# Six more weight units get their low parts by an accumulating DMA, and the causal weights are loaded later

## The chip, the cores and the metric

The kernel runs on one core of one Trainium2 chip. The metric is the device time of one execution in microseconds (us). Engines are called by these names: PE or TensorE (matmul), DVE or VectorE, ACT or ScalarE, POOL or GpSimd, SP or SyncE (here only a queue that issues DMAs).

## What is computed

Two layers of an autoregressive decoder trunk, for 512 prompt positions and 8 single-step samples side by side (T = 520 columns), 1024 channels. Layer 0 is a conv module, layer 1 a chunked gating module; after each comes `x <- LayerNorm(alpha * x + sublayer(x))`. What matters here is the end of layer 0 and the start of layer 1:

```python
# end of layer 0
y = concat([a, bo]) * silu(g)
out = einsum('bld,de->ble', y, w_out_ab)          # second half of it: z_p
x = layer_norm(alpha * x + out, ln_g[0], ln_b[0])
# layer 1
z = einsum('bld,de->ble', x, w_in_c)
u, v, g = split(z)
u = gelu(u); v = layer_norm(gelu(v))
w_causal = w_s * tril(ones((128, 128)))           # the causal weights, 8 heads
mix = einsum('hts,bnshd->bnthd', w_causal, v_in_chunks) + b_s
y = u * mix * silu(g)
out = einsum('bld,de->ble', y, w_out_c)
x = layer_norm(alpha * x + out, ln_g[1], ln_b[1])
```

## The kernel before

Activations lie with channels on the 128 partitions: eight tiles of 128 x 520 for 1024 channels. All matmul operands are split in two float32r parts, a high one (rounded) and a low one (what the rounding left), and each product is three matmuls: hi x hi, lo x hi, hi x lo. So 8 channel tiles (k) by 3 make the 24 matmuls of one output tile of 128 x 260.

The weights come as "units" of 1024 x 128, 512 KB each, in the order of use, through `unit(n)`, which loads ahead up to five units (`LEAD`). `load_unit` (lines 116 to 129) does for each: SP issues the load of `raw` (three buffers), ScalarE makes the high part `whi` (L121), and the low part `wlo` is made in one of two ways. Either VectorE subtracts `raw - whi` (L128), or, for units in the set `BY_DMA` (10 to 49 before), ScalarE writes `-raw`, rounded, into `wlo` (L125) and GpSimd issues a DMA that reads the unit from memory a second time and adds it to `wlo` on the way (L126). `whi` and `wlo` lie in 12 buffers, six units; units 70 and 71 lie in the buffers of tag `M` instead.

The place of this change:

- Units 64 to 71 are the last part of layer 0's output projection (`z_p`). `out_part` (line 478) runs over them twice, first for columns 0 to 259, then for columns 260 to 519, called at lines 587 and 588. In it, for each of eight output tiles, VectorE adds the sums to the residue `r` (L492) and with that frees the PSUM bank. After the fourth, a matmul with ones (`shift`, L502) gives a first mean, which VectorE subtracts from all eight `r` (L504); squares (ScalarE L507) and sums follow, and `norm()` closes it: means by matmul (L384, L385, `mean` and `sqs`), L536 to L538 for the reciprocal deviation, L544, L566, ScalarE's L567. `split_x1` (line 577) makes the parts `x1h` (ScalarE L582) and `x1l` (VectorE L583) for layer 1. The first columns' norm lies beside the second columns' matmuls.
- Units 72 to 77 are the first six v units of layer 1 (`NVF` = 6). They are also done twice: `z_v{i}_0` for the first columns (line 627), which lies beside the second columns' norm, then `z_v{i}_1` (line 633). Both take PSUM banks in turn with `z_p`, by `one()`. Units 78 to 87 are the other v units, over all columns at once.
- Between the two stands the code for the causal weights: loads of `wt` and `bs` by GpSimd's queue, the causal mask (`affine_select`), and the split into `wth` and `wtl` on GpSimd. `wth` and `wtl` are first read by the matmuls `rows` (L674), `wt` by `mix` (L718), `bs` by VectorE's L713; all come after the v units.

The order of the instructions on each engine is set by a scheduler from the program's order, its own model of durations, and the priorities in the code (`soon()`, `background()`); each engine then runs its list in order. GpSimd's list holds its DMA issues too.

Of the kernel before, what the change touches and what calls it, by code (L numbers as in the profile page):

```python
# [9 lines left out]
F32 = mybir.dt.float32  # L10
F32R = mybir.dt.float32r
BF16 = mybir.dt.bfloat16
AF = mybir.ActivationFunctionType
ALU = mybir.AluOpType
AX = mybir.AxisListType

P = 128
D = 1024
E2 = 2048
SEQ = 512  # L20
# [8 lines left out]
NH = 8  # L29
# [21 lines left out]
def decoder_kernel(  # L51
# [19 lines left out]
    nc = tc.nc  # L71
# [3 lines left out]
    wpool = ctx.enter_context(tc.tile_pool(name="wpool", bufs=1))  # L75
# [9 lines left out]
    def y_slot(dt, name, n=T):  # L85
        return slots.tile([P, n], dt, tag="Y", name=name, bufs=17)

    def ab_slot(name):
        return slots.tile([P, T], F32, tag="AB", name=name, bufs=8)
# [7 lines left out]
    def zt(name):  # L97
        return zps.tile([P, 2, 512], F32, tag="z", name=name)

    def mt(name):  # L100
        return mps.tile([P, 512], F32, tag="m", name=name)

    def zh(z):
        return z[:, :, :TH]

    def two(t):
        return t.rearrange("p (a b) -> p a b", a=2)

    def hs(h):
        return slice(h * TH, (h + 1) * TH)  # L110
# [5 lines left out]
    def load_unit(wtag=("W", 12)):  # L116
# [5 lines left out]
        lo = wpool.tile([P, KT, P], F32R, tag=wtag[0], name=f"wlo_{n}", bufs=wtag[1])  # L122
        if n in BY_DMA:

# [4 lines left out]
        units.append((hi, lo))  # L129


    BY_DMA = set(range(10, 50))
    EXTRA = set()
    for base in (64, 128):
        EXTRA.update((base + 6, base + 7))
# [1 line left out]
    def unit(n):  # L137
        while len(units) < min(n + 1 + LEAD, n_units):
            load_unit(("M", 4) if len(units) in EXTRA else ("W", 12))
        return units[n]  # L140

    def mm(ps, w, ah, al, c):
        hi, lo = w
        for k in range(KT):
            for j, (a, b) in enumerate(((hi, ah), (lo, ah), (hi, al))):
                nc.tensor.matmul(  # L146
                    ps,
                    a[:, k, :],
                    b[k][:, c],
                    start=(k == 0 and j == 0),  # L150
                    stop=(k == KT - 1 and j == 2),
                )

    def halves(z):
        return [z[:, h, :] for h in range(2)]

    def mm2(z, w, ah, al):
        hi, lo = w
        for k in range(KT):
            for h in range(2):  # L160
                for j, (a, b) in enumerate(((hi, ah), (lo, ah), (hi, al))):
                    nc.tensor.matmul(  # L162
                        z[h][:, :TH],
                        a[:, k, :],
                        b[k][:, hs(h)],
                        start=(k == 0 and j == 0),
                        stop=(k == KT - 1 and j == 2),
                    )
# [15 lines left out]
    for k in range(KT):  # L184
# [5 lines left out]
        q, j = k // 4, k % 4  # L190
# [64 lines left out]
    def one(j, name):  # L255
        if j % 2:
            return zt(name)[:, 0, :]
        return cps.tile([P, SEQ], F32, tag="cv", name=name)
# [29 lines left out]
    for i in range(KT):  # L288
# [64 lines left out]
        op=ALU.mult,  # L353
# [5 lines left out]
    with background():  # L359
        for j in range(2):  # L360
# [6 lines left out]
                op=ALU.mult,  # L367
# [209 lines left out]
    def split_x1(d, c0, c1):  # L577
# [11 lines left out]
    n += KT  # L589


    wt = wpool.tile([P, NH, P], F32, tag="M", name="wt", bufs=4)
    nc.gpsimd.dma_start(wt, wsT_in)
    bs = wpool.tile([P, NH, P], F32, tag="M", name="bs", bufs=4)
    nc.gpsimd.dma_start(bs, bs_in)

    nc.gpsimd.affine_select(
        wt, wt, pattern=[[0, NH], [1, P]], compare_op=ALU.is_ge, fill=0.0, base=0, channel_multiplier=-1
    )

    wth, wtl = [], []
    for j in range(2):
        w = wt[:, 4 * j : 4 * j + 4, :].rearrange("p a b -> p (a b)")
        wth.append(y_slot(F32R, f"wth_{j}", SEQ))
        wtl.append(y_slot(F32R, f"wtl_{j}", SEQ))
        nc.gpsimd.tensor_copy(wth[j], w)
        nc.gpsimd.tensor_tensor(wtl[j], w, wth[j].bitcast(F32), op=ALU.subtract)

    NV = 2 * KT
    NVF = 6  # L610
    vt = [None] * NV
# [4 lines left out]
    def v_tok(i):  # L616
        nc.gpsimd.tensor_copy(vs[:, i, :], vt[i][:, SEQ:])
        m = mt(f"vt_{i}")
        for c in range(NC):
            nc.tensor.transpose(m[:, c * P : (c + 1) * P], vt[i][:, c * P : (c + 1) * P], ident)  # L620
        t = ab_slot(f"vtok_{i}") if i < 8 else slots.tile([P, T], F32, tag="SB", name=f"vtok_{i}", bufs=8)
        nc.scalar.copy(t[:, :SEQ], m)
        for c in range(NC):
            nc.vector.bn_stats(stats[:, c, i, :], t[:, c * P : (c + 1) * P])
        vtok[i] = t
# [7 lines left out]
    for i in range(NVF):  # L633
        z = one(i, f"z_v{i}_1")[:, :TH]
        mm(z, unit(n + i), x1h, x1l, hs(1))
        t = vt[i]
        with tc.issue_after(last_act[0]):
            nc.scalar.activation(t[:, hs(0)], t[:, hs(0)], AF.Gelu_apprx_tanh)
        nc.scalar.activation(t[:, hs(1)], z, AF.Gelu_apprx_tanh)
        if i > 0:  # L640
            v_tok(i - 1)
    for i in range(NVF, NV):
        z = zt(f"z_v{i}")
        mm2(halves(z), unit(n + i), x1h, x1l)
        vt[i] = y_slot(F32, f"v_{i}")
        nc.scalar.activation(two(vt[i]), zh(z), AF.Gelu_apprx_tanh)
        v_tok(i - 1)
# [244 lines left out]
```

## Time and profile before

| what | us |
|---|---|
| median of 3 runs | 834.26 (833.76 to 834.76) |
| the profiled execution | 834.73 |
| its span, first to last instruction | 833.0 |
| TensorE busy | 814.2 (98%) |
| VectorE busy | 536.6 (64%) |
| ScalarE busy | 347.2 (42%) |
| GpSimd busy | 88.0 (11%) |

Rows of the profile read: place in the span or source line, engine, operation, what is written from what, shapes, count, then busy us and mean ns. In the list of waits: who waited, for whom, total us, times, longest. In a timeline: start, length, and in brackets the idle time ahead of it and what ended it. TensorE overlaps its matmuls, so the time per matmul is read from one start to the next, not from the length of one.

### The profile page before, as it was taken

Reading aid. Unit: us, or ns where it says so; the run is one execution under the profiler, and the core shown is the slowest. Engines: PE = TensorE matmul, PEld = TensorE weight load, DVE = VectorE, ACT = ScalarE, POOL = GpSimd, SP = SyncE. Lnnn points to the kernel's source line nnn. Section 1 sums busy time; section 2 is a strip of 40 time slices with the busy share of each in tenths; the row PEclk is TensorE's granted clock in tenths of the full one; section 3 lists DMA queues with packets and bytes.
Section 4 is the critical chain, followed back from the end, with each engine's and each line's share of the span. In section 5 each row is a group of like instructions: output and inputs, shape, how many; then the busy total and the mean of one; then the engine's idle time right before and its main releaser. Section 6 shows DMA issues by size and latency. Waiting matters only on the chain.

```text
span 833.0 us, 16028 instructions
## 1 busy us (share of the span) xinstructions
PE 814.2 (98%) x6792; PEld 812.2 (98%) x6792; DVE 536.6 (64%) x914; ACT 347.2 (42%) x510; POOL 88.0 (11%) x158
## 2 busy tenths in 40 slices
PE   8999999999999999999989999999999999999994
PEld 8999999999999999999979999999999999999993
DVE  5899998999962576446885432596355433526566
ACT  5545454455354444442647423323432133334243
POOL 0121221221110000000021111100000000000032
PEclk9999999999999999999989999999999999999997
DMA  8798988889888543231331432214233223222011
GB/s 290 208 206 191 209 185 185 184 191 216 182 173 189 167 115 102 79 124 52 84 119 51 128 85 93 77 56 126 78 87 92 84 94 102 77 87 92 1 53 52
DMA packets 32873, 103.37 MB, mean 124 GB/s; under 512 B 4209, under 2 KB 7937, under 8 KB 32801
## 3 DMA queue, kind: packets, MB, share of 16 engines
q1 hardware_dynamic: 26000, 79.01, 32.2%
q0 software_dynamic: 6800, 23.33, 15.0%
q8 instruction: 53, 0.87, 0.4%
q14 instruction: 20, 0.16, 0.1%
HBM read 98.89 MB, written 3.44 MB: 123 GB/s over the span
## 4 chain that ended last, share of the span: by engine, by line
PE 96%; DMA 1%; DVE 1%; ACT 0%; SPq 0%; issue 0%; ACTq 0%; DVEq 0%
PE z_p L146 11%; PE z_gc L162 11%; PE z_u L162 11%; PE z_v L162 7%; PE z_q L162 6%; PE z_o L162 6%; PE z_c L162 5%; PE z_ga L162 5%; PE z_post L162 5%; PE z_h L162 5%; PE z_gb L162 5%; PE z_val L162 5%; PE z_gate L162 5%; PE z_v L146 5%; PE mix L718 2%; PE vt L620 1%
## 5 line engine op out<-in xcount | busy, mean ns | idle before, releaser
L121 ACT CAST whi<-raw 128x1024 fp32r<-128x1024 f32 x134 | 139.9, 1048 | 324.9 <-PE z_u L162 44.9
L128 DVE TENSOR_TENSOR wlo<-raw,whi 128x1024 fp32r<-128x1024 f32 x94 | 114.4, 1224 | 142.5 <-ACT whi L121 141.9
L274 DVE SCALAR_TENSOR_TENSOR acc<-apad,pa,acc 128x512 f32<-128x512 f32 x240 | 165.7, 751 | 3.6 <-ACT acc L271 2.7
L162 PE MATMUL z_gc<-x1h,whi 128*128 128x260 f32 x256 | 72.9, 285 | 0.0
L162 PE MATMUL z_u<-x1h,whi 128*128 128x260 f32 x256 | 72.4, 283 | 0.0
L162 PE MATMUL z_gc<-x1h,wlo 128*128 128x260 f32 x256 | 72.0, 281 | 0.0
L162 PE MATMUL z_u<-x1l,whi 128*128 128x260 f32 x256 | 72.0, 281 | 0.0
L162 PE MATMUL z_gc<-x1l,whi 128*128 128x260 f32 x256 | 72.0, 281 | 0.0
L162 PE MATMUL z_u<-x1h,wlo 128*128 128x260 f32 x256 | 72.0, 281 | 0.0
L126 POOL DMA_DIRECT2D wlo<-in_wu x40 | 34.7, 869 | 139.2 <-ACT wlo L125 132.2
L162 PEld LDWEIGHTS z_u<-x1h,wlo 128*128 128x128 f32 x256 | 48.1, 188 | 0.1
L162 PEld LDWEIGHTS z_gc<-x1h,wlo 128*128 128x128 f32 x256 | 48.2, 188 | 0.0
L162 PEld LDWEIGHTS z_gc<-x1l,whi 128*128 128x128 f32 x256 | 48.1, 188 | 0.0
L162 PEld LDWEIGHTS z_u<-x1h,whi 128*128 128x128 f32 x256 | 48.0, 188 | 0.1
L162 PEld LDWEIGHTS z_u<-x1l,whi 128*128 128x128 f32 x256 | 48.1, 188 | 0.0
L162 PEld LDWEIGHTS z_gc<-x1h,whi 128*128 128x128 f32 x256 | 48.1, 188 | 0.0
L162 PE MATMUL z_v<-x1h,whi 128*128 128x260 f32 x160 | 46.0, 287 | 0.0
L162 PE MATMUL z_v<-x1h,wlo 128*128 128x260 f32 x160 | 45.0, 281 | 0.0
L162 PE MATMUL z_v<-x1l,whi 128*128 128x260 f32 x160 | 45.0, 281 | 0.0
L125 ACT ACTIVATE wlo<-raw 128x1024 fp32r<-128x1024 f32 x40 | 42.2, 1055 | 0.0
L162 PE MATMUL z_c<-xh,wlo 128*128 128x260 f32 x128 | 36.1, 282 | 0.3 <-DVE wlo L128 0.3
L146 PE MATMUL z_p<-yh_c,whi 128*128 128x260 f32 x128 | 36.3, 284 | 0.0
(260 smaller groups left out, 2723.4 us busy)
## 6 DMA issues: line engine op xcount, KB each, us to landing
raw<-in_wu SPq DMA_DIRECT2D x134, 512.0 KB, 3.9
wlo<-in_wu POOLq DMA_DIRECT2D x40, 512.0 KB, 7.7
xr<-in_xT SPq DMA_DIRECT2D x8, 260.0 KB, 4.2
x<-in_xT SPq DMA_DIRECT2D x7, 260.0 KB, 5.1
out_y<-r SPq DMA_DIRECT2D x8, 130.0 KB, 1.7
out_y<-out SPq DMA_DIRECT2D x4, 260.0 KB, 2.2
raw_s<-in_w SPq DMA_DIRECT2D x8, 128.0 KB, 4.5
xs<-in_cache_a SPq DMA_DIRECT2D x2, 496.0 KB, 8.2
```

What stands on the lines that cost most here:

```text
L121: nc.scalar.copy(hi, raw)
L125: nc.scalar.mul(lo, raw, -1.0)
L126: nc.gpsimd.dma_start(lo, wu[n - 2], accum_op=ALU.add)
L128: nc.vector.tensor_tensor(lo, raw, hi.bitcast(F32), op=ALU.subtract)
L146: nc.tensor.matmul(ps, a[:, k, :], b[k][:, c], start=(k == 0 and j == 0), stop=(k == KT - 1 and j == 2),)
L162: nc.tensor.matmul(z[h][:, :TH], a[:, k, :], b[k][:, hs(h)], start=(k == 0 and j == 0), stop=(k == KT - 1 and j == 2),)
L274: nc.vector.scalar_tensor_tensor(acc[i], apads[i][:, j : j + SEQ], pa[:, i, PA_W + j : PA_W + j + 1], acc[i], op0=ALU.mult, op1=ALU.add,)
L620: nc.tensor.transpose(m[:, c * P : (c + 1) * P], vt[i][:, c * P : (c + 1) * P], ident)
L718: nc.tensor.matmul(m[:, c * P : (c + 1) * P], vtok[i][:, c * P : (c + 1) * P], wt[:, h, :], start=True, stop=True)
```

## The change

Two edits. Units 72 to 77 join the set `BY_DMA`: their low parts are written by ScalarE and the accumulating DMA, no longer by VectorE. And the block that loads, masks and splits the causal weights moves from ahead of the v units to behind the sixth of them.

```diff
-    BY_DMA = set(range(10, 50))
+    BY_DMA = set(range(10, 50)) | set(range(72, 78))
...
-    wt = wpool.tile([P, NH, P], F32, tag="M", name="wt", bufs=4)
-    nc.gpsimd.dma_start(wt, wsT_in)
-    bs = wpool.tile([P, NH, P], F32, tag="M", name="bs", bufs=4)
-    nc.gpsimd.dma_start(bs, bs_in)
-    nc.gpsimd.affine_select(
-        wt, wt, pattern=[[0, NH], [1, P]], compare_op=ALU.is_ge, fill=0.0, base=0, channel_multiplier=-1
-    )
-    wth, wtl = [], []
-    for j in range(2):
...
-        nc.gpsimd.tensor_copy(wth[j], w)
-        nc.gpsimd.tensor_tensor(wtl[j], w, wth[j].bitcast(F32), op=ALU.subtract)
     NV = 2 * KT
...
         if i > 0:
             v_tok(i - 1)
+    (the same block, unchanged, between the two loops over v units)
     for i in range(NVF, NV):
```

The lists of the engines change with it. In the rows below a number behind a name tells one buffer's use from another's: `r_3519`, `3578`, `3637`, `3698`, `3757`, `3816`, `3875`, `3934` are the eight residues 0 to 7, and `_260` marks the second columns.

VectorE, from the fourth L492 of the second columns to the subtraction of `shift`. Before:

```order
L492 TENSOR_TENSOR r_3698<-z_p_260_3_4943,r_3698 128x260
L497 TENSOR_TENSOR tot_260_4914<-tot_260_4914,r_3637 128x260
L128 TENSOR_TENSOR wlo_4721<-raw_4717,whi_4719 128x1024
L128 TENSOR_TENSOR wlo_4757<-raw_4753,whi_4755 128x1024
L583 TENSOR_TENSOR x1l_4817<-r_3519,x1h_4816 128x260
L497 TENSOR_TENSOR tot_260_4914<-tot_260_4914,r_3698 128x260
L583 TENSOR_TENSOR x1l_4823<-r_3578,x1h_4822 128x260
L128 TENSOR_TENSOR wlo_5189<-raw_5185,whi_5187 128x1024
L583 TENSOR_TENSOR x1l_4829<-r_3637,x1h_4828 128x260
L583 TENSOR_TENSOR x1l_4835<-r_3698,x1h_4834 128x260
L583 TENSOR_TENSOR x1l_4841<-r_3757,x1h_4840 128x260
L583 TENSOR_TENSOR x1l_4847<-r_3816,x1h_4846 128x260
```

VectorE from the same L492 in the change:

```order
L492 TENSOR_TENSOR r_3698<-z_p_260_3_4948,r_3698 128x260
L497 TENSOR_TENSOR tot_260_4919<-tot_260_4919,r_3698 128x260
L583 TENSOR_TENSOR x1l_4822<-r_3519,x1h_4821 128x260
L504 TENSOR_TENSOR r_3757<-r_3757,shift_260_4975 128x260
L504 TENSOR_TENSOR r_3816<-r_3816,shift_260_4975 128x260
L504 TENSOR_TENSOR r_3519<-r_3519,shift_260_4975 128x260
L504 TENSOR_TENSOR r_3578<-r_3578,shift_260_4975 128x260
L504 TENSOR_TENSOR r_3637<-r_3637,shift_260_4975 128x260
L504 TENSOR_TENSOR r_3698<-r_3698,shift_260_4975 128x260
L504 TENSOR_TENSOR r_3875<-r_3875,shift_260_4975 128x260
L504 TENSOR_TENSOR r_3934<-r_3934,shift_260_4975 128x260
L492 TENSOR_TENSOR r_3757<-z_p_260_4_4996,r_3757 128x260
```

The low parts are gone, one `x1l` (L583) instead of seven stands ahead of the last L504s, and the L492 of the fifth output tile follows them at once.

ScalarE, from the first `x1h` of the first columns (L582) to the first squares of the second (L507). Before:

```order
L582 CAST x1h_4816<-r_3519 128x260
L567 ACTIVATE r_3637<-r_3637,pa 128x260
L567 ACTIVATE r_3698<-r_3698,pa 128x260
L567 ACTIVATE r_3757<-r_3757,pa 128x260
L567 ACTIVATE r_3816<-r_3816,pa 128x260
L567 ACTIVATE r_3875<-r_3875,pa 128x260
L567 ACTIVATE r_3934<-r_3934,pa 128x260
L582 CAST x1h_4822<-r_3578 128x260
L121 CAST whi_5187<-raw_5185 128x1024
L582 CAST x1h_4828<-r_3637 128x260
```

ScalarE at the same place in the change (`whi_4759` and `wlo_4761` are unit 76, `whi_5179` and `wlo_5181` unit 77):

```order
L567 ACTIVATE r_3875<-r_3875,pa 128x260
L582 CAST x1h_4821<-r_3519 128x260
L567 ACTIVATE r_3934<-r_3934,pa 128x260
L121 CAST whi_4759<-raw_4757 128x1024
L125 ACTIVATE wlo_4761<-raw_4757 128x1024
L121 CAST whi_5179<-raw_5177 128x1024
L125 ACTIVATE wlo_5181<-raw_5177 128x1024
L582 CAST x1h_4827<-r_3578 128x260
L507 ACTIVATE sq_260_0_4985<-r_3519 128x260
L507 ACTIVATE sq_260_1_4987<-r_3578 128x260
```

The first `x1h` now stands behind seven L567 and the casts and negated copies of units 72 to 75; two more units stand between it and the second `x1h`. Five L507 more follow before the third `x1h`.

TensorE, from the last `z_p` rows on. Before:

```order
L502 MATMUL shift_260_4970<-tot_260_4914,ones_h 128x260
L146 MATMUL z_p_260_7_5081<-yh_a_4483,wlo_4562 128x260
L146 MATMUL z_p_260_7_5081<-yl_a_4484,whi_4560 128x260
L146 MATMUL z_v_0_5184<-x1h_4816,whi_4593 128x260
L146 MATMUL z_v_0_5184<-x1h_4816,wlo_4595 128x260
L146 MATMUL z_v_0_5184<-x1l_4817,whi_4593 128x260
L146 MATMUL z_v_0_5184<-x1h_4822,whi_4593 128x260
```

TensorE at the same place in the change:

```order
L146 MATMUL z_p_260_7_5086<-yl_a_4484,whi_4560 128x260
L146 MATMUL z_v_0_5176<-x1h_4821,whi_4593 128x260
L146 MATMUL z_v_0_5176<-x1h_4821,wlo_4595 128x260
L146 MATMUL z_v_0_5176<-x1l_4822,whi_4593 128x260
L146 MATMUL z_v_0_5210<-x1h_4821,whi_4648 128x260
L146 MATMUL z_v_0_5210<-x1h_4821,wlo_4650 128x260
L146 MATMUL z_v_0_5210<-x1l_4822,whi_4648 128x260
L146 MATMUL z_v_0_5243<-x1h_4821,whi_4684 128x260
L146 MATMUL z_v_0_5243<-x1h_4821,wlo_4686 128x260
L146 MATMUL z_v_0_5243<-x1l_4822,whi_4684 128x260
L146 MATMUL z_v_0_5176<-x1h_4827,whi_4593 128x260
```

`shift` has moved up behind the fifth row of the seventh output tile (44 places before the first `z_v` row), and the `z_v` rows of units 72 to 75 are mixed: first all rows that need only the first channel tile, then those of the second. GpSimd's list now holds the six accumulating DMAs of units 72 to 77, then three copies of `vs`, then the loads of `wt` and `bs`, and the mask and split between further copies of `vs`.

More of the change, by code (lines that the diff above doesn't have):

```diff
@@ L589, in decoder_kernel @@
     n += KT
-    wt = wpool.tile([P, NH, P], F32, tag="M", name="wt", bufs=4)
-    nc.gpsimd.dma_start(wt, wsT_in)
-    bs = wpool.tile([P, NH, P], F32, tag="M", name="bs", bufs=4)
-    nc.gpsimd.dma_start(bs, bs_in)
-    nc.gpsimd.affine_select(
-        wt, wt, pattern=[[0, NH], [1, P]], compare_op=ALU.is_ge, fill=0.0, base=0, channel_multiplier=-1
-    )
-    wth, wtl = [], []
-    for j in range(2):
-        w = wt[:, 4 * j : 4 * j + 4, :].rearrange("p a b -> p (a b)")
-        wth.append(y_slot(F32R, f"wth_{j}", SEQ))
-        wtl.append(y_slot(F32R, f"wtl_{j}", SEQ))
-        nc.gpsimd.tensor_copy(wth[j], w)
-        nc.gpsimd.tensor_tensor(wtl[j], w, wth[j].bitcast(F32), op=ALU.subtract)
     NV = 2 * KT
@@ L641, in decoder_kernel @@
             v_tok(i - 1)
+    wt = wpool.tile([P, NH, P], F32, tag="M", name="wt", bufs=4)
+    nc.gpsimd.dma_start(wt, wsT_in)
+    bs = wpool.tile([P, NH, P], F32, tag="M", name="bs", bufs=4)
+    nc.gpsimd.dma_start(bs, bs_in)
+    nc.gpsimd.affine_select(
+        wt, wt, pattern=[[0, NH], [1, P]], compare_op=ALU.is_ge, fill=0.0, base=0, channel_multiplier=-1
+    )
+    wth, wtl = [], []
+    for j in range(2):
+        w = wt[:, 4 * j : 4 * j + 4, :].rearrange("p a b -> p (a b)")
+        wth.append(y_slot(F32R, f"wth_{j}", SEQ))
+        wtl.append(y_slot(F32R, f"wtl_{j}", SEQ))
+        nc.gpsimd.tensor_copy(wth[j], w)
+        nc.gpsimd.tensor_tensor(wtl[j], w, wth[j].bitcast(F32), op=ALU.subtract)
     for i in range(NVF, NV):
```

## The prediction

> **What bounds the kernel now.** I read the page's first lines, then who waited for whom on TensorE, then the chain that ended last, and only then the single engines around the one place where TensorE stood still.
>
> ```profile
> span 833.0 us, 16028 instructions
> PE 814.2 (98%) x6792; PEld 812.2 (98%) x6792; DVE 536.6 (64%) x914; ACT 347.2 (42%) x510; POOL 88.0 (11%) x158
> ...
> PE z_v L146 <- DVE r L492: 4.1, 1, 4.1
> PE z_first L212 <- ACT xh L205: 1.2, 2, 1.0
> ```
>
> TensorE is busy 98% of the span, so an edit off TensorE can only win what TensorE waits. After the start there is one wait of size: the first matmul of `z_v` (unit 72) waits 4.1 us for VectorE's L492, which reads the last `z_p` sums out of the PSUM bank that `z_v` takes over. The chain there, in us from the span's start:
>
> ```profile
> 420.00 0.45 PE shift L502 x2
> 420.48 1.10 DVE r L504 x3
> ...
> 421.91 1.68 DVE r L504 x5
> ...
> 424.27 0.43 DVE r L492
> ...
> 424.83 7.07 PE z_v L146 x34
> ```
>
> TensorE runs out of `z_p`, VectorE then does eight L504 subtractions and the L492 behind them, and `z_v` starts at 424.83. The single matmuls (start, length) and three windows (span, then TensorE, weight load, VectorE, ScalarE, GpSimd busy; granted clock) show a second price:
>
> ```profile
> 420.40 0.28 PE L146 MATMUL z_p<-yl_a,whi 128*128 128x260 f32 x1
> 424.83 0.56 PE L146 MATMUL z_v<-x1h,whi 128*128 128x260 f32 x1 [4.15 <-DVE r L492]
> ...
> 431.01 0.29 PE L146 MATMUL z_v<-x1h,wlo 128*128 128x260 f32 x1
> ...
> 399.60:420.40 20.80, 20.80 (x175) 20.74 (x173) 19.03 (x37) 14.83 (x25) 1.10 (x2) 1.00 0.49 142
> 424.80:431.00 6.20, 6.17 (x28) 6.20 (x29) 6.06 (x14) 1.90 (x5) 2.71 (x3) 0.50 0.00 0
> 433.50:445.40 11.90, 11.90 (x101) 11.90 (x100) 8.62 (x21) 7.38 (x18) 0.00 (x0) 1.00 0.00 0
> ```
>
> From 433.5 on, a matmul takes 11.90/101 = 0.118 us of TensorE. After the stall the granted clock is 0.50: the 28 matmuls from 424.83 to 431.01 took 6.18 us where 28 x 0.118 = 3.30 would do, 2.88 lost. The stall itself lost 424.83 - 420.40 - 0.118 = 4.31. So this place costs 4.31 + 2.88 = 7.19 us, the most that the change can win here. In the window before it VectorE is busy 19.03 of 20.80 us: it is the late engine, and these groups say with what (busy us, mean ns, 399.7 to 424.8):
>
> ```profile
> L128 DVE TENSOR_TENSOR wlo<-raw,whi 128x1024 fp32r<-128x1024 f32 x6 | 7.2, 1218 | 1.0 <-ACT whi L121 0.5 <-PE z_p L146 0.5
> L504 DVE TENSOR_TENSOR r<-r,shift 128x260 f32<-128x260 f32 x8 | 2.9, 421 | 0.1
> ```
>
> **The change, part 1: six subtractions leave VectorE.** These six L128 are exactly units 72 to 77. Without their 7.2 us I walk VectorE's new order, with the lengths of before:
>
> ```profile
> 402.41 2.77 DVE L544 TENSOR_TENSOR r<-r,mean 128x260 f32<-128x260 f32 x8
> 405.09 0.42 DVE L492 TENSOR_TENSOR r<-z_p,r 128x260 f32<-128x260 f32 x1
> 405.43 1.77 DVE L538 RECIPROCAL rstd<-rstd 128x260 f32<-128x260 f32 x1
> 409.99 2.81 DVE L566 TENSOR_TENSOR r<-r,rstd 128x260 f32<-128x260 f32 x8
> ```
>
> Up to the reciprocal's end (407.1) nothing moves but one subtraction that fitted in a gap. Then L492, L495, eight L566 (2.81) and three more of about 0.35: VectorE is through at 411.7. Next is the first x1l, which needs ScalarE, then the L504s, which need the `shift` matmul. In the new order `shift` stands 44 places before the first `z_v` row instead of three, so it ends 43 x 0.118 before 420.52 (where `z_v` can start, 420.40 + 0.118), at 415.45. Eight L504 at the pace of the eight L544 (2.77) end at 418.2, the L492 that frees the bank at 418.7. Before it ended at 424.7. TensorE comes at 420.52: 1.8 us to spare, the stall goes, and with it the half clock.
>
> **Part 2: ScalarE gets six negated copies (L125).** Prices and what it has to do there:
>
> ```profile
> L125 ACT ACTIVATE wlo<-raw 128x1024 fp32r<-128x1024 f32 x40 | 42.2, 1055 | 0.0
> ...
> 408.69 1.05 ACT L121 CAST whi<-raw 128x1024 fp32r<-128x1024 f32 x1 [1.82 <-PE z_p L146]
> 412.13 1.05 ACT L121 CAST whi<-raw 128x1024 fp32r<-128x1024 f32 x1 [0.58 <-DMA raw<-in_wu]
> 413.39 3.08 ACT L567 ACTIVATE r<-r,pa 128x260 f32<-128x260 f32 x6
> 417.63 1.96 ACT L582 CAST x1h<-r 128x260 fp32r<-128x260 f32 x6
> ...
> 422.28 1.09 ACT L507 ACTIVATE sq<-r 128x260 f32<-128x260 f32 x3 [0.26 <-DVE r L504]
> ```
>
> Six by 1.05 is 6.3 us more, and ScalarE was busy 14.83 of 20.80. The first three fit in its waits for `z_p`. Then: the cast of unit 75 at 408.69 as before (it waits for TensorE), its L125 to 410.7, seven L567 (3.08/6 each) to 414.3, the first x1h to 414.7 (VectorE's x1l to 415.1, just ahead of `shift`), the last L567 to 415.1, cast and L125 of 76 and of 77, four by 1.0, to 419.1, the second x1h to 419.4, seven L507 by 0.36 to 421.9, the third x1h to 422.3. TensorE wants the second x1h at its tenth `z_v` row (420.52 + 9 x 0.118 = 421.6) and the third at the 25th (423.35): 2.2 and 1.1 us to spare. This is the tightest cover in the change; gone, it costs TensorE the excess, one for one.
>
> **Part 3: six accumulating DMAs on GpSimd's queue,** and the raw buffers that come free by L125 instead of L128. Issue and landing, of the 40 low parts and then of the 134 raw loads:
>
> ```profile
> L126 POOL DMA_DIRECT2D wlo<-in_wu x40: 854/866/906, 40.0 to 260.8; - x40
> ...
> DMA to landing us min/median/max: 7.3/7.7/9.1
> ...
> DMA to landing us min/median/max: 3.4/3.9/9.0
> ```
>
> GpSimd is idle there. Units 72 to 74 have their L125 done by 407.8, so the last lands by 407.8 + 0.9 + 9.1 = 417.8 at worst; `z_v` rows want it at 421.2. Unit 75: 410.7 + 10.0 = 420.7, wanted at the 20th row, 422.8. Units 76 and 77 land by 429.1; they are wanted 100 and more rows in, from 432. The raw load of unit 77 reuses unit 74's buffer: issued 407.8, landed by 416.8 at worst, wanted at 417.1. All hidden, by 0.3 to 3 us even with the longest landing seen, so I put the cost at nothing. SP's queue keeps its order; two of its raw loads start earlier.
>
> **Part 4: the causal weights move** behind the sixth `z_v` pair. Two loads and five GpSimd operations, two of them below; beside them VectorE's row took 1.52 us where its like takes 0.42:
>
> ```profile
> 422.29 1.10 POOL L597 TENSOR_SCALAR_AFFINE_SELECT wt<-wt 128x1024 f32<-128x1024 f32 x1 [3.63 <-DMA wt<-in_wsT]
> ...
> 424.15 1.32 POOL L607 TENSOR_TENSOR wtl<-wt,wth 128x512 fp32r<-128x512 f32 x1
> ...
> 426.35 1.52 DVE L514 TENSOR_TENSOR tot<-r,r 128x260 f32<-128x260 f32 x1
> ```
>
> [...] The move takes this off the second norm and puts it beside the splits of units 78 to 80. There is room:
>
> ```profile
> 451.45 2.54 DVE L128 TENSOR_TENSOR wlo<-raw,whi 128x1024 fp32r<-128x1024 f32 x2 [4.41 <-ACT whi L121]
> ...
> 464.89 0.24 PE z_v L162 x2
> 532.98 0.23 PE rows L674
> ```
>
> Unit 78's low part is ready by 454.0 and used at 464.89; the five operations are some 5 us in all. The weights are first used at 532.98. What queues behind the load on GpSimd are small copies of `vs`, wanted only after the last v unit. Were VectorE held for all of it, unit 78 would still be ready 5.8 us ahead; so 0 at both ends.
>
> **Part 5: the second norm, behind `z_v`.** If TensorE is 7 us earlier, the second halves are wanted earlier too:
>
> ```profile
> 433.30 0.29 PE L385 MATMUL sqs<-parts_ssq,ones_r 128*128 128x260 f32 x1
> 440.68 0.40 ACT L582 CAST x1h<-r 128x260 fp32r<-128x260 f32 x1
> ```
>
> From the last `sqs` matmul to the first x1h's end is 7.8 us. In the new order `sqs` is 76 rows behind the first `z_v` row (429.5), and the second halves' first row 148 behind (438.0); 429.5 + 7.8 = 437.3. That is 0.7 to spare without counting that the subtractions now stand before `sqs`. Cost nothing, at most about 0.5.
>
> **Sum.** -4.31 - 2.88 = -7.19, nothing given back. The profiled execution took 834.73 (833.0 in the span), so 827.5; the median of the three runs, 834.26, gives 827.1. I say 827.3. [...]
>
> **The rivals.** (1) ScalarE becomes the bound: the second and third x1h wait behind the casts and L125 of 76 and 77. For: it is my tightest cover, 1.1 us. Against: all its waits are for TensorE or for loads with room. ScalarE 2 to 4 us late leaves a wait of 1 to 3; the wait of 1.0 at the start left the clock whole, so the time is 828.3 to 830.3. (2) No change, since the wait only gets another name: the first x1l stands ahead of the L504s on VectorE and waits for ScalarE. It would have to come 5 us after 415.1 to bring the old start back: 833 to 835. Against: no row of ScalarE ahead of it waits for anything that the change delays. (3) Slower: TensorE takes its rows in order, so one late low part, unit 74's at the eighth row, blocks all. It decides from 421.3 on, 13.5 us after its L125; to end slower it would have to stop TensorE for over 6 us plus the half clock, landing some 20 us after its issue, twice the longest of 40: 836.5.
>
> **Chances.** Forecast 0.78; (1) 0.11; a little more gain than 7.2, to 826.4 and below, 0.04; (2) 0.04; (3) 0.03. The three runs before lie within 0.5 of their median, so the forecast's own range is 826.6 to 828.0. For 8 in 10 and the bounds above I take 826.5 to 829.6. About 0.2% (1.7 us) is what a measurement of this kernel can tell from no change: faster by more 0.92, within 0.05, slower 0.03.
>
> **What would show it.** Right: the wait of `z_v` for L492 gone, granted clock 1.00 from 420 to 431, L492 on unit 68's sums ending near 418.7, x1h number two near 419.4, span about 826. Wrong, if TensorE waits for x1h or a low part between 421 and 424, or in the second halves near 438; then the wait's name tells which cover was missing.

## The result, and the profile after

The changed kernel takes 828.17 us (median of four runs, 827.44 to 828.85), the kernel before 834.01 beside it: a ratio of 0.993 (95% interval 0.9912 to 0.9947), 5.8 us less. A second series later gave 827.55 against 834.08, a ratio of 0.9923 (0.9906 to 0.9939), 6.5 us less. The forecast was 827.3, with 826.5 to 829.6 as the range. Of its narrower range for the forecast alone, 826.6 to 828.0, the first series lies 0.2 us outside and the second inside.

First the busy time by engine, from the page of the changed kernel:

```profile
span 827.1 us, 16038 instructions
PE 812.5 (98%) x6792; PEld 810.9 (98%) x6792; DVE 528.6 (64%) x908; ACT 352.0 (43%) x516; POOL 92.0 (11%) x164
```

VectorE has six instructions fewer, ScalarE and GpSimd six more each. These are all the waits of TensorE that the changed kernel's trace lists (engine and line, what it waited for, total us, times, longest):

```profile
PE warm L175 <- DVE warm L172: 1.1, 1, 1.1
PE z_first L212 <- ACT xh L205: 0.9, 1, 0.9
PE z_c L162 <- DVE wlo L128: 0.5, 1, 0.5
```

All three lie in the first 19 us. The wait of 4.1 for L492 is gone and no other has its place. The single matmuls around it (start, length):

```profile
421.15 0.28 PE L146 MATMUL z_p<-yl_a,whi 128*128 128x260 f32 x1
421.26 0.28 PE L146 MATMUL z_v<-x1h,whi 128*128 128x260 f32 x1
...
422.35 0.28 PE L146 MATMUL z_v<-x1h,whi 128*128 128x260 f32 x1
```

`z_v` follows `z_p` as one `z_p` row follows another. The windows of before, in the changed kernel (TensorE, weight load, VectorE, ScalarE, GpSimd; clock, share of the DMA engines, GB/s):

```profile
399.60:420.40 20.80, 20.80 (x174) 20.74 (x174) 14.78 (x39) 17.75 (x24) 4.36 (x5) 1.00 0.83 201
421.20:427.40 6.20, 6.20 (x54) 6.20 (x54) 6.18 (x18) 4.83 (x16) 0.82 (x1) 1.00 1.07 274
433.50:445.40 11.90, 11.90 (x101) 11.90 (x100) 5.95 (x17) 10.73 (x26) 0.00 (x0) 1.00 0.01 1
```

The second holds 54 matmuls in 6.20 us where 28 stood, at clock 1.00. VectorE went from 19.03 busy to 14.78 in the first, ScalarE from 14.83 to 17.75, and the DMA engines from 0.49 to 0.83 and from 0.00 to 1.07.

The local gain is read between two points of the chain that ended last (start, us). Of the kernel before, the start; the first L162 row of `z_v`, 464.89, is shown in the prediction:

```profile
18.23 1.82 PE z_c L162 x13
```

Of the changed kernel both:

```profile
18.95 1.12 PE z_c L162 x7
...
458.53 0.24 PE z_v L162 x2
```

This execution began its main work 0.72 us later than the one before, which neither edit touches (the first `z_c` row, one ahead of the rows shown, started at 17.07 to 18.50 in the 14 profiles of this study, in no order by kernel). Between the two points it took 464.89 - 458.53 + 0.72 = 7.08 us less; 7.19 were predicted for this pair. Of these the whole execution kept 833.0 - 827.1 + 0.72 = 6.6. About 0.2 went between that `z_v` row and the last `z_p` row of layer 1, where all six profiles without the move took 354.4 us and seven of the eight with it 354.6 (the eighth, with three units, waited there); the rest went behind the last matmul. No run shows the cause of either.

### The profile page after: what moved, and what is told of

Same layout as the page of the kernel before. It is cut to its first block, busy times and chain, and to the rows that moved or that the text cites. A ratio compares the mean times of both kernels' runs of the same rounds, so it can differ in the third digit from the quotient of the medians.

```text
span 827.1 us, 16038 instructions
## 1 busy us (share of the span) xinstructions
PE 812.5 (98%) x6792; PEld 810.9 (98%) x6792; DVE 528.6 (64%) x908; ACT 352.0 (43%) x516; POOL 92.0 (11%) x164
## 4 chain that ended last, share of the span: by engine, by line
PE 96%; DMA 1%; DVE 1%; ACT 0%; SPq 0%; issue 0%; ACTq 0%; DVEq 0%
PE z_p L146 11%; PE z_gc L162 11%; PE z_u L162 11%; PE z_v L162 7%; PE z_q L162 6%; PE z_o L162 6%; PE z_c L162 6%; PE z_ga L162 6%; PE z_post L162 6%; PE z_h L162 6%; PE z_gb L162 6%; PE z_val L162 5%; PE z_gate L162 5%; PE z_v L146 4%; PE mix L718 2%; PE vt L603 1%
## 5 line engine op out<-in xcount | busy, mean ns | idle before, releaser
L128 DVE TENSOR_TENSOR wlo<-raw,whi 128x1024 fp32r<-128x1024 f32 x88 | 108.1, 1233 | 140.9 <-ACT whi L121 140.9
L162 PE MATMUL z_gc<-x1h,whi 128*128 128x260 f32 x256 | 72.9, 285 | 0.0
L126 POOL DMA_DIRECT2D wlo<-in_wu x46 | 40.0, 869 | 294.4 <-ACT msq L530 140.3
L162 PE MATMUL z_u<-x1h,whi 128*128 128x260 f32 x256 | 72.4, 283 | 0.0
L162 PE MATMUL z_gc<-x1h,wlo 128*128 128x260 f32 x256 | 72.0, 281 | 0.0
L162 PE MATMUL z_u<-x1l,whi 128*128 128x260 f32 x256 | 72.0, 281 | 0.0
L162 PE MATMUL z_gc<-x1l,whi 128*128 128x260 f32 x256 | 72.0, 281 | 0.0
L162 PE MATMUL z_u<-x1h,wlo 128*128 128x260 f32 x256 | 72.0, 281 | 0.0
L125 ACT ACTIVATE wlo<-raw 128x1024 fp32r<-128x1024 f32 x46 | 48.5, 1055 | 0.0
L162 PEld LDWEIGHTS z_u<-x1h,wlo 128*128 128x128 f32 x256 | 48.1, 188 | 0.1
L162 PEld LDWEIGHTS z_gc<-x1h,wlo 128*128 128x128 f32 x256 | 48.1, 188 | 0.0
L162 PEld LDWEIGHTS z_u<-x1h,whi 128*128 128x128 f32 x256 | 48.0, 188 | 0.1
L162 PEld LDWEIGHTS z_gc<-x1l,whi 128*128 128x128 f32 x256 | 48.1, 188 | 0.0
L162 PEld LDWEIGHTS z_u<-x1l,whi 128*128 128x128 f32 x256 | 48.1, 188 | 0.0
L162 PEld LDWEIGHTS z_gc<-x1h,whi 128*128 128x128 f32 x256 | 48.1, 188 | 0.0
L162 PE MATMUL z_v<-x1h,whi 128*128 128x260 f32 x160 | 46.0, 287 | 0.0
L162 PE MATMUL z_v<-x1l,whi 128*128 128x260 f32 x160 | 45.0, 281 | 0.0
L162 PE MATMUL z_v<-x1h,wlo 128*128 128x260 f32 x160 | 45.0, 281 | 0.0
L162 PE MATMUL z_c<-xh,wlo 128*128 128x260 f32 x128 | 36.1, 282 | 0.5 <-DVE wlo L128 0.5
```

The lines of the kernel that those rows point to most:

```text
L125: nc.scalar.mul(lo, raw, -1.0)
L126: nc.gpsimd.dma_start(lo, wu[n - 2], accum_op=ALU.add)
L128: nc.vector.tensor_tensor(lo, raw, hi.bitcast(F32), op=ALU.subtract)
L162: nc.tensor.matmul(z[h][:, :TH], a[:, k, :], b[k][:, hs(h)], start=(k == 0 and j == 0), stop=(k == KT - 1 and j == 2),)
```

## The experiments

Two theories stood against each other. A: the six subtractions alone made TensorE wait, so that the edit of `BY_DMA` does everything and the move of the causal weights nothing. B: the move has a share of its own, since it takes GpSimd's operations off the second norm. Beside them the two terms of the sum, the pause and the half clock, were to be taken apart.

**One half of the change at a time.** The low parts by DMA alone:

```diff
-    BY_DMA = set(range(10, 50))
+    BY_DMA = set(range(10, 50)) | set(range(72, 78))
```

> Units 72 to 77 by the accumulating DMA, but the causal weights loaded and split where they were before. Theory A (VectorE's six subtractions alone made the stall): no wait of z_v for L492, clock 1.00, local gain about 7, time 827.5 to 828.7. Rival B (the move is needed): GpSimd's 5 us of masking and splitting lie beside the second norm, VectorE's x1l rows and sums stretch as L514 did before (1.52 for 0.42), TensorE waits 1 to 3 us for x1l or mean: 829 to 831.

Measured: 827.6 us (827.49 to 827.87) against 834.13, ratio 0.992 (0.9906 to 0.9935). GpSimd's list, then a window of all engines:

```profile
427.71 1.10 POOL L597 TENSOR_SCALAR_AFFINE_SELECT wt<-wt 128x1024 f32<-128x1024 f32 x1 [7.27 <-DMA wt<-in_wsT]
...
429.58 1.30 POOL L607 TENSOR_TENSOR wtl<-wt,wth 128x512 fp32r<-128x512 f32 x1
```

```profile
420.00:433.00 13.00, 13.00 (x111) 13.00 (x110) 11.60 (x30) 7.04 (x21) 5.30 (x6) 1.00 0.82 243
```

GpSimd's mask and splits lie beside the second norm and TensorE is busy through all of it at clock 1.00. So the whole gain is there without the move. The other half:

```diff
-    wt = wpool.tile(...)          # ahead of NV
...
+    wt = wpool.tile(...)          # behind the loop over the first six v units
...
```

> Only the causal weights are moved; the low parts of 72 to 77 stay on VectorE. Theory A: the wait of z_v for L492 stays at 3.7 to 4.2 us with the half clock behind it, 833.3 to 834.5, no measurable change. Rival B: the move matters by itself; VectorE's rows beside GpSimd's (0.84 for 0.42 before) get short, the wait falls to about 3.3 us; if that is short enough for the clock to stay whole, 830.5.

Measured: 834.09 (832.77 to 834.82, ten runs), ratio 0.9996 (0.9987 to 1.0005): no change. The wait is the old one, 0.2 to 0.3 us shorter:

```profile
425.69 0.56 PE L146 MATMUL z_v<-x1h,whi 128*128 128x260 f32 x1 [3.88 <-DVE r L492]
...
428.86 0.30 PE L146 MATMUL z_v<-x1l,whi 128*128 128x260 f32 x1
```

A stands, B falls. But the half clock ended at 428.86, 3.2 us after the start of `z_v`, not 6.2: the second term of the sum was not what it had seemed.

**Two units instead of six**, with the move:

```diff
+    BY_DMA = set(range(10, 50)) | set(range(72, 74))
```

> Only units 72 and 73 by the accumulating DMA (and the move). VectorE keeps four subtractions, and 2 x 1.2 us leave it. Theory A: the wait of z_v for L492 shrinks from 4.15 to 1.4 to 2.0 us. If the clock stays whole after such a pause: gain 4.31 - 1.7 + 2.88 = 5.5, 828.7. If any pause longer than 1.0 halves the clock: gain 2.6, 831.5. If VectorE's time isn't the cause, the wait stays near 4: 834.

Measured: 831.25 (830.62 to 831.46), ratio 0.9962 (0.9948 to 0.9977). The wait was 2.09, just above the 1.4 to 2.0 expected. Two subtractions fewer (2 x 1.22 = 2.4 us) took about 2 us off the wait, and the clock was still halved, for 3.5 us:

```profile
422.24 0.47 PE L146 MATMUL z_v<-x1h,whi 128*128 128x260 f32 x1 [2.09 <-DVE r L492]
```

**The half clock by itself.** The kernel before, with small matmuls on spare data in the pause (`warm` of the start, result unused):

```diff
-    out_part(n, TH, T, yh, yl, res, LN0_G, split_x1)()
+    norm2 = out_part(n, TH, T, yh, yl, res, LN0_G, split_x1)
+    with tc.issue_after(last_mm[0]):
+        fill = mt("fill")
+        for j in range(64):
+            nc.tensor.matmul(fill[:, :P], warm, warm, start=True, stop=True)
+    norm2()
```

> The kernel before, with 64 matmuls of the warm-up's kind (128 x 128, bf16, results unused) put on TensorE behind the last z_p row, in the pause. L492 still comes at 424.7. Theory A (2.88 us of the 7.19 are the half clock, brought on by the pause): the clock stays whole, z_v starts at 424.8 as before, time 831.0 to 831.5, gain 2.9. Rival: the half clock has another cause (load, a fixed time): 834, or some 835 when the fillers run at half rate and end after L492.

Measured: 831.44 (830.79 to 832.6, seven runs), ratio 0.9966 (0.9955 to 0.9978), 2.7 us less than the kernel before. TensorE's rows (line numbers are three higher in this kernel), and a window behind them:

```profile
419.40 3.75 PE L595 MATMUL fill<-warm 128*128 128x128 bf16 x64
423.69 0.36 PE L149 MATMUL z_v<-x1h,whi 128*128 128x260 f32 x1 [0.54 <-DVE r L495]
```

```profile
424.00:431.00 7.00, 7.00 (x60) 7.00 (x59) 6.39 (x14) 2.77 (x9) 2.40 (x3) 1.00 0.00 0
```

`z_v` comes as late as ever (423.69 - 419.40 = 4.3 us after the last `z_p` row), but at the whole clock. So the half clock alone is worth 2.7 us of the 5.8 to 6.5, and the pause the rest.

**Each kernel again**, unedited, for the spread between executions.

> The changed kernel once more, beside others on one chip. The pause and the half clock are gone, so only the start should vary from run to run: all runs within about 0.8 of their median, 827.5 to 828.5, and the same as with the low parts by DMA alone. If the move of the causal weights costs or wins something, the two differ by more than 0.5.

Measured: the second series above, 827.55 (827.38 to 827.69).

> The kernel before, unchanged, for a second profile. The kernels with the weights moved and with two units showed 3 us of half clock behind the pause, the first profile of this kernel 6.2. If the length hangs on the execution and not on the kernel: the pause for L492 again 4.0 to 4.3, the half clock anywhere from 2.9 to 6.2 us, costing 1.3 to 2.9. If 6.2 belongs to this kernel's longer pause: 6.0 to 6.4 again.

Measured: 834.42 us. The wait was 4.6, and the half clock held for 28 matmuls, 424.55 to 430.71, as in the first profile.

**Three units.**

```diff
+    BY_DMA = set(range(10, 50)) | set(range(72, 75))
```

> Units 72 to 74 by the accumulating DMA, 75 to 77 on VectorE. By the walk of lengths the L492 that frees the bank ends at 421.4 to 421.9 where z_v could start at 420.5: a pause of 0.9 to 1.4 us. Pauses of 0.5 and 1.0 left the clock whole, 2.1 halved it. Clock whole: 828.3 to 829.2. Clock halved: another 1.3 to 2.9, 830 to 831.5. If VectorE's time isn't what z_v waits for, the pause stays at 2 or more.

Measured: median 829.49, ratio 0.9952 (0.9937 to 0.9967), but the ten runs lie from 828.16 to 832.79, 4.6 us apart, where two units gave 0.8 and six 0.3 to 1.4. The profiled run took 832.59. Its rows of VectorE, ScalarE and TensorE around the start of `z_v`:

```profile
419.25 1.21 DVE L128 TENSOR_TENSOR wlo<-raw,whi 128x1024 fp32r<-128x1024 f32 x1
420.38 0.42 DVE L583 TENSOR_TENSOR x1l<-r,x1h 128x260 fp32r<-128x260 f32 x1
420.72 0.42 DVE L492 TENSOR_TENSOR r<-z_p,r 128x260 f32<-128x260 f32 x1
...
412.16 0.39 ACT L582 CAST x1h<-r 128x260 fp32r<-128x260 f32 x1
...
420.80 0.39 ACT L582 CAST x1h<-r 128x260 fp32r<-128x260 f32 x1
...
421.29 0.36 PE L146 MATMUL z_v<-x1h,whi 128*128 128x260 f32 x1 [0.59 <-ACT x1h L582]
```

`z_v` came 0.8 us late, at clock 1.00. The profile names an x1h, because one ended last before it, at 421.19; but that is the eighth. The first `z_v` row reads the first x1h, which ended at 412.55, and takes over the PSUM bank that L492 frees. That L492 ended at 421.14, behind the last of the three subtractions left on VectorE. So this is the old wait again, a little under the 0.9 to 1.4 expected and with the clock whole behind it; it is not rival 1. The second place in the same execution, by the chain:

```profile
451.23 7.63 DMA raw<-in_wu
...
458.93 1.04 ACT whi L121
459.98 0.50 ACT vtok L605
...
460.52 0.44 PE vt L603 x2
```

This raw load ran beside the two moved loads of the causal weights and took 7.63 us; ScalarE stood for 4.35 and TensorE for 2.0. Behind that pause the clock was halved as well:

```profile
460.50:461.50 1.00, 0.98 (x9) 0.99 (x9) 1.00 (x3) 0.79 (x3) 0.69 (x2) 1.00 0.35 139
...
462.50:464.00 1.50, 1.50 (x9) 1.50 (x8) 1.50 (x3) 0.75 (x2) 1.50 (x2) 0.50 0.69 243
```

So the first place cost 0.8, the second about 2.2 and 1.6 for the half clock, 4.6 in all, and with the second place the time of this run fits neither expectation; 832.59 less 4.6 is 828.0, where the shortest of the ten runs lies (828.16). What the runs between met isn't known.

**The six subtractions on GpSimd**, no DMA, with the move:

```diff
-            nc.vector.tensor_tensor(lo, raw, hi.bitcast(F32), op=ALU.subtract)
+            eng = nc.gpsimd if 72 <= n < 78 else nc.vector
+            eng.tensor_tensor(lo, raw, hi.bitcast(F32), op=ALU.subtract)
```

> The low parts of 72 to 77 by plain subtraction on GpSimd, no second DMA and no negated copy on ScalarE, weights moved as in the change. Theory A (any relief of VectorE does it): six by about 2.6 us on an idle engine, no pause, 827.5 to 828.5. Rival (the two engines hold each other up when both read two inputs): VectorE's rows between 401 and 420 stretch by up to the 15.7 us of GpSimd's, the wait for L492 stays at 3 or more, 833 to 838.

Measured: 828.85 (828.81 to 829.75), ratio 0.9942 (0.9927 to 0.9957), a little above what theory A expected and far from the rival's 833. `z_v` doesn't wait, but `shift` does, for 0.8. VectorE and GpSimd in this kernel (lines one higher):

```profile
407.57 6.91 DVE L567 TENSOR_TENSOR r<-r,rstd 128x260 f32<-128x260 f32 x8
```

```profile
404.59 7.57 POOL L129 TENSOR_TENSOR wlo<-raw,whi 128x1024 fp32r<-128x1024 f32 x3 [1.61 <-ACT whi L121]
```

These eight multiplications by `rstd`, which take 2.81 us alone (L566 before), took 6.91 beside GpSimd's subtractions. So the DMA isn't needed for the gain either: what counts is that the work leaves VectorE. But the GpSimd way gives some of it back through VectorE.

**How long the half clock lasts.** 6.2, 6.2, 3.2 and 3.5 us had been seen behind pauses of 2 to 4.7. Either the pause sets the length (P) or something of the single execution does (Q). Four more executions, without edits but for the last, which is the filler with 24 matmuls in place of 64.

> The kernel of e2 once more, for the length of the half clock behind the pause. Length set by the pause (theory P): a pause of about 3.9 us leaves a half clock of about 2.9 us as in e2, since 3.9 gave 2.9 and the 4.15 and 4.6 of the kernel before gave 6.2. Set by something of the single execution (rival Q): the same pause, but another length, 6.2 for instance.

> The kernel of e3 once more. P: pause 2.1 us, half clock 3.3 us again. Q: another length behind the same pause, or none.

> The kernel before, a third profile. P: pause 4.1 to 4.6 us, half clock 6.2 us. Q: another length, near 3.

> The kernel before, with 24 extra matmuls on spare data in the pause instead of 64 (their result is not used). They take some 1.4 us, so the pause that is left is 2.6 to 3.0 us. P: by the two units of e3 (2.1 gave 3.3) and e2 (3.9 gave 2.9), a half clock of about 3 us, and the time 1.5 us under the kernel before's. Q: a half clock of any length up to 6.2 us, or none.

Measured, in this order: 834.27, 830.5, 833.86 and 832.52 us, beside 834.26 of the kernel before. Windows of the third profile of before (columns as above), ahead of, in and behind the half clock:

```profile
424.80:425.60 0.80, 0.78 (x6) 0.80 (x7) 0.80 (x2) 0.67 (x2) 0.80 (x2) 1.00 0.00 0
425.90:428.80 2.90, 2.90 (x15) 2.90 (x15) 2.90 (x6) 0.81 (x2) 1.61 (x2) 0.50 0.00 0
429.20:431.00 1.80, 1.80 (x18) 1.80 (x17) 1.66 (x6) 0.41 (x1) 0.00 (x0) 1.00 0.00 0
```

`z_v` starts at the whole clock, is halved 0.8 us later, with TensorE busy, and is whole again 3.4 us after that. The two units again:

```profile
421.60:422.50 0.90, 0.85 (x7) 0.88 (x8) 0.90 (x4) 0.69 (x2) 0.00 (x0) 1.00 0.00 0
422.80:425.70 2.90, 2.90 (x15) 2.90 (x15) 2.79 (x10) 1.22 (x3) 0.00 (x0) 0.50 0.00 0
426.10:429.10 3.00, 3.00 (x27) 3.00 (x26) 1.19 (x3) 1.01 (x3) 0.00 (x0) 1.00 0.02 5
```

The pauses of about 2 us and more, from the single matmuls and the granted clock of each trace. The pause runs from the end of the last row's 0.118 us (or of the filler) to the next row; "lost" is the time from the first row behind it to the end of the half clock, less 0.118 for each matmul in it.

| kernel | pause, us | half clock, from first row behind it | lost, us |
|---|---|---|---|
| before | 4.3 | at once, to 6.2 after it | 2.9 |
| before, second | 4.7 | at once, to 6.2 | 2.9 |
| move only, again | 3.9 | at once, to 5.8 | 2.7 |
| move only | 4.0 | at once, to 3.2 | 1.5 |
| two units | 2.3 | at once, to 3.5 | 1.6 |
| before, third | 4.2 | from 0.8 to 4.2 | 1.6 |
| two units, again | 2.0 | from 1.0 to 4.4 | 1.7 |
| filler of 24 | 2.8 | from 0.8 to 4.2 | 1.6 |
| three units, at `vt` | 2.2 | from 1.3 to 4.7 | 1.6 |

The same kernel shows different lengths (before: 6.2 and 3.4; the move: 3.2 and 5.8), so P falls and Q stands. The granted clock as each trace records it gives the lengths more exactly: counted from its own change, and not from the first row, the half clock lasted 3.41 us in six of the nine and 6.83 in three (before, first: 424.13 to 430.96), and the stretch at the whole clock ahead of it in that profile, 419.84 us, is 123 times 3.413. Steps of that length can be counted back from a change of the clock. In the step just ahead of a half clock TensorE was idle for 1.96 of 3.41 us (two units, again); in one behind which the clock stayed whole for one more step it was idle for 1.60 (before, third, 418.81 to 422.22). With 0.23 us of the pause in its first step the half clock ended behind that step (the move alone, 425.46 to 428.87); with 0.70 it lasted for one more (before, first). So the author's reading of these nine traces is that the clock changed only at the ends of such steps, and that the share of a pause in each made it one step of half clock or two. No run was made to test it.

## Why the prediction was right, point by point

Times of the changed trace are 0.74 us later here than in the prediction's frame, for the late start; the numbers below are compared with that added.

**Part 1** held to 0.1 us. VectorE in the changed kernel:

```profile
415.24 0.43 DVE L583 TENSOR_TENSOR x1l<-r,x1h 128x260 fp32r<-128x260 f32 x1 [2.83 <-ACT x1h L582]
416.32 2.77 DVE L504 TENSOR_TENSOR r<-r,shift 128x260 f32<-128x260 f32 x8 [0.65 <-PE shift L502]
419.01 1.09 DVE L492 TENSOR_TENSOR r<-z_p,r 128x260 f32<-128x260 f32 x3
```

The first of the three L492 ends near 419.4, predicted 418.7 + 0.74. TensorE comes at 421.26: 1.8 us to spare, as said.

**Part 2** held in its outcome, with half the margin. ScalarE:

```profile
416.56 1.06 ACT L125 ACTIVATE wlo<-raw 128x1024 fp32r<-128x1024 f32 x1
418.85 1.05 ACT L121 CAST whi<-raw 128x1024 fp32r<-128x1024 f32 x1 [1.23 <-DMA raw<-in_wu]
419.80 1.06 ACT L125 ACTIVATE wlo<-raw 128x1024 fp32r<-128x1024 f32 x1
420.76 0.39 ACT L582 CAST x1h<-r 128x260 fp32r<-128x260 f32 x1
421.06 2.28 ACT L507 ACTIVATE sq<-r 128x260 f32<-128x260 f32 x7
423.24 0.39 ACT L582 CAST x1h<-r 128x260 fp32r<-128x260 f32 x1
```

The second x1h ended at 421.15 (predicted 420.14), wanted at 422.35; the third at 423.63 (423.04), wanted at 424.1. To spare were 1.2 and 0.5 us, not 2.2 and 1.1. The cause is the wait of 1.23 for the raw load of unit 77, which is a step of part 3.

**Part 3** failed in its bound: "landed by 416.8 at worst" became 418.8, after the 0.74 some 1.3 us later than the longest landing seen before allowed. Landings (min, median, max) of the raw loads, then of the low parts, between 404 and 430 of the changed trace:

```profile
DMA to landing us min/median/max: 8.7/9.3/11.1
...
DMA to landing us min/median/max: 8.9/9.4/11.3
```

The bounds of 9.0 and 9.1 came from loads issued at 43 us, where the low parts of units 10 to 49 are made and the DMA engines' share is 0.89 (40 to 260 us; 0.99 from 43 to 52). Here it is 0.96 from 404 to 416 and 1.05 from 416 to 428 (0.42 and 0.61 at this place before), so the share alone doesn't tell the two places apart. But three low parts are issued within 5.1 us here (406.65 to 411.73), each with a raw load beside it, and landed after 8.9, 10.4 and 11.3; there it was two within 3.5 (39.96 and 43.43), and the third came at 49.63. That this crowding makes the loads longer is an estimate from these rows; no run tested it. It cost TensorE nothing because the third x1h still had 0.5 us to spare. With three units a raw load of 9.08 us held ScalarE for 1.74 at the same place, and TensorE didn't wait for it there either.

**Part 4** was right that the move costs next to nothing in the changed kernel (at most the 0.2 us above), but its "0 at both ends" looked only at VectorE. The moved loads meet the raw loads of later units: in the changed trace ScalarE waits twice for one,

```profile
455.40 1.05 ACT L121 CAST whi<-raw 128x1024 fp32r<-128x1024 f32 x1 [1.79 <-DMA raw<-in_wu]
458.76 1.05 ACT L121 CAST whi<-raw 128x1024 fp32r<-128x1024 f32 x1 [1.55 <-DMA raw<-in_wu]
```

where it waited for none before (and once, for 1.46, with the low parts alone). The slowest raw load between 444 and 466 us took 4.2 to 5.1 us in the four profiles of before and of the low parts alone, and 6.1 to 8.9 in all eight with the move. With three units this stopped TensorE for 2.0 us. The low-parts edit alone, without the move, is as fast as the change: 827.6 and 827.55. (The GpSimd operation beside VectorE's row of 1.52 was the second L607, at 426.31 for 1.28, not the one that the prediction shows.)

**Part 5** held: the first x1h of the second columns ended at 435.5, 3 us ahead of the row that wants it at 438.7, more than the 0.7 predicted.

**The sum.** -4.31 for the pause is right. -2.88 for the half clock was a single execution's: it measured 2.9, 2.9 and 1.6 in three profiles of the same kernel, and the filler, which takes it away alone, gained 2.7. The step that failed is taking the 6.18 us of the one trace for the length of the half clock: one trace can't decide a length that changes from one execution to the next, and this one happened to show the long form. With 1.6 to 2.9 the gain is 5.9 to 7.2 us; the two series measured 5.8 and 6.5. The first series also holds the late start of its profiled run (828.85, the slowest of the four).

**The rivals.** None occurred in the changed kernel. (1): ScalarE was late by 0.6 to 1.0 us, but its tightest cover kept 0.5. (2), no change by another name: the first x1h ended at 415.2, before `shift`. (3): the low parts landed late too, but TensorE's list of waits has none for them.

## What to carry to other kernels

When TensorE is busy 98% of the span, look for the one engine that is late at the one wait, and move work off that engine alone; where it goes matters less (a DMA gained 6.5, GpSimd 5.2) as long as it doesn't hold up the same engine there (beside GpSimd's subtractions eight rows of VectorE took 6.91 us, 2.81 alone). Behind nine pauses of TensorE of 2.0 to 4.7 us here the half clock lost another 1.5 to 2.9: count it on top, and take it from several profiles. A landing time measured where two accumulating DMAs were issued within 3.5 us (at most 9.0 for the raw load, 9.1 for the low part) was no bound for the place where the change issues three within 5.1 (11.1 and 11.3): ask first how many will be under way at once there.

## What was not expected of the hardware

- The half clock can begin after TensorE has resumed: 0.8 to 1.3 us later behind four of nine pauses, and it then lasts 3.4 us. A pause of 2.0 us was enough for it; the gap of 0.8 in the kernel with three units (421.29 - 420.41, less one row) left the clock whole, and so did the gap ahead of `shift` with the subtractions on GpSimd, where the wait was 0.8.
- A 512 KB load that takes 3.9 us at the median took 8.7 to 11.1 us with the DMA share at 0.96 to 1.05 and accumulating DMAs of the same size beside it.
- VectorE's eight multiplications by `rstd` (128 x 260) were 0.93 us long each at the mean beside GpSimd's subtractions, 0.43 alone.
